# Own places for modulation rows in an FFN output, a new product order, and gate sums in place, in a two-layer diffusion step

## The chip, the cores and the metric

The kernel runs on one core of one Trainium2 chip. The metric is the device time of one execution in microseconds (us), as a median over several runs. The kernel before took 1518.62 us (three runs, 1517.99 to 1518.99).

A core has five engines with queues of their own, each worked off in order. TensorE multiplies matrices (PE in the profile; PEld is its weight load, which overlaps). VectorE (DVE) does element-wise work with two operands, ScalarE (ACT) copies and activation functions, GpSimd (POOL) side work, and SyncE (SP) issues transfers. POOL issues transfers too, on a queue of its own. Engines wait for each other through semaphores. SBUF is the on-chip memory from which the engines work, PSUM the eight banks into which TensorE accumulates.

## The reference

Two layers run over 512 latent tokens and 128 prompt tokens (640 together, T), with a model width of 1024 (D). Layer 0 mixes with MLA heads and neighbourhood attention, layer 1 with grouped-query attention (GQA, 8 heads). After each mixer comes a SwiGLU FFN with a hidden width of 2816. A condition vector scales, shifts and gates every sub-layer; there are two conditions, one for the latent and one for the prompt tokens:

```python
m = silu(cond) @ w_mod[l] + b_mod[l]          # 6 x 1024: sh1 sc1 g1 sh2 sc2 g2
h  = rms_norm(x, norm_mix[l]) * (1 + sc1) + sh1
x  = x + g1 * mixer(h)
h  = rms_norm(x, norm_ffn[l]) * (1 + sc2) + sh2
gate, up = split(h @ w_ffn_in[l], 2)
x  = x + g2 * ((silu(gate) * up) @ w_ffn_out[l])
```

The output is the final RMS norm of x for both groups, and the context tensors of each layer.

## The kernel before

**Precision and layout.** Activations lie transposed: features on the 128 partitions, the 640 tokens along the free dimension, in two halves of 320 (HT). Weights and activations are split into a high and a low part (ScalarE copies the high part, VectorE subtracts it for the low part), and a product is three matmuls: high x high, high x low, low x high (`mm3`). So every weight tile costs a load, a ScalarE pass and a VectorE pass before TensorE can finish with it.

**FFN input** (`ffn`, from L1238, the loop from L1497). The hidden width has 22 blocks (fb) of 128. After the first two blocks, each block is one step of a seven-product scheme for two-by-two block matrices (halves of the features, halves of the tokens), with sums of weights (X, Y, Z, W, built from the gate weights g and the up weights u by the class `Weights`) and sums of activations (D, N, C, E, built by `ModS`). TensorE's order in a block is X x first half, D, E of the block before, N, X x second half, Z, C; VectorE follows with `up`, `g` (a PSUM sum that must be read before E adds to that bank), the weight sums s, the low parts and the gating. In layer 0, from block 5 on (QUICK), the transfer itself adds the two halves of the gate weights; for blocks 2 to 4 VectorE adds them. Gate weights of blocks 2 to 4 are loaded into `rawp`, later ones into tiles with the tag "wr" (two buffers, 1536 columns in layer 0), which before that hold normalised activations of `ModS`.

**FFN output.** Part one (from L1608) handles the first ten hidden blocks for the eight output blocks n of 128 features; the three hidden blocks that never left SBUF run ahead for n = 0 to 3. Each n then has two jobs (`jobs`, L1645), and `prepare` loads, splits and queues the weights of the next job (`wout`, L1608). The raw weights go in turn into `rawp` (three buffers) and into one buffer in the pool fo. Part two (from L1677) handles the other twelve hidden blocks in six pairs, again with seven products for each pair p of output blocks: S2, A11, S3, A12 and A22 for the left (first) half of the tokens and S1 and S4 for the right. The weight sums S1 and S2 lie in tiles of fo with the tags "S1" and "S2" (768 columns). PLAN is TensorE's order, MAKE that in which weights are made, three products ahead. The activations of the hidden pairs (kinds T1 to T4, B11, B21, B22) were spilled to DRAM; `later` are those fetched during part one, the rest follows into `spots` as the buffers of part one come free.

**Modulation rows.** Most of the modulation is not done by TensorE. `left` lists 56 rows of 128 output features; for each, 512 KB of weights are fetched and VectorE multiplies them with the two conditions (two instructions "junk", L1841, of 1024 columns, with a running sum). `mod_side` spreads these rows over the kernel as side work: its plan gives the number of rows for each stage, "o" in the mixer's output projection (after each output block), "fb" in the FFN input (after each block) and "n" in the FFN output part one. `fetch` takes the next rows and issues their loads (SP's queue in the FFN input and in the heads, POOL's queue elsewhere); the next `step` queues their products on VectorE behind the instruction it is given, then fetches the rows for the next step. Without a place of its own, a row's raw weights take one of the three buffers of `rawp`, which the weights use too. In the GQA heads, `gside.ask(1)` (L2120) brings one row to a head.

**Order of the work.** The kernel is written for a scheduler that fixes each engine's instruction order when it is built; the program's order and `after`/`issue_after` constrain it. On the chip an engine runs its queue in that order, and an instruction that waits holds up all behind it. A buffer's next user waits for its last reader.

Of the kernel before, what the change touches and what calls it, by code (L numbers as in the profile page):

```python
# [11 lines left out]
F32 = mybir.dt.float32  # L12
# [6 lines left out]
P = 128  # L19
# [31 lines left out]
def body(ctx, tc, xT, vecs, wm0, wm0g, wm1, wA, wNV, wNA, wMK, wMV, wOA, wGQ, wGK, wGV, wOC,  # L51
# [1186 lines left out]
    def ffn(l, x, pend, hm, nxt, side, opened):  # L1238
# [98 lines left out]
        def fetch_g(fb):  # L1337
            if fb >= FB:
                return
            g = wFI[l, fb, 0]  # L1340
            if fb == FEW or l == 0 and fb < QUICK:
                raws[fb, 0] = load(g, 1024, f"wg{l}_{fb}r")
                return
            t = raws[fb, 0] = fp.tile([P, WR[l]], F32, tag="wr", bufs=2, name=f"wg{l}_{fb}r")
            if l == 1:
                nc.sync.dma_start(t, g)
                return
            y = t[:, :1024].rearrange("p (a b) -> p a b", a=2)

            def from_(at, step):  # L1350
                return bass.AP(tensor=g.tensor, offset=g.offset + at, ap=[list(g.ap)[0], [step, 2], [1, 512]])
            nc.sync.dma_start(y, from_(0, 0))
            nc.gpsimd.dma_start(y, from_(512, P * 1024 - 512), accum_op=ALU.add)
            nc.sync.dma_start(t[:, 1024:], g[:, 512:])

        class Weights:

            def __init__(self, fb):
                self.fb = fb
                self.u, g = raws[fb, 1], raws[fb, 0]  # L1360
                self.g0, self.g, self.s13 = g[:, :512], g[:, 512:1024], None
                if l == 0 and fb >= QUICK:
                    self.g, self.s13 = g[:, 1024:], g[:, :1024]
                self.X = wX[fb - FEW] if fb < FEW + AHEAD else None

            def sums(self):
                ru, s13 = self.u, self.s13
                if s13 is None:
                    tag, n, bufs = ("ws", 1024, 2) if l else ("w4", 1024, 2) if self.fb == FEW else ("wr", WR[0], 2)
                    s13 = fp.tile([P, n], F32, tag=tag, bufs=bufs, name=f"s13{l}_{self.fb}")[:, :1024]  # L1370
                    dve(V.tensor_tensor, s13[:, :512], self.g0, self.g, ALU.add)
                    dve(V.tensor_tensor, s13[:, 512:], ru[:, :512], self.g0, ALU.add)
                s24 = fp.tile([P, 1024], F32, tag="ws", bufs=1 + l, name=f"s24{l}_{self.fb}")
                dve(V.tensor_tensor, s24[:, :512], s13[:, 512:], self.g, ALU.add)
                dve(V.tensor_tensor, s24[:, 512:], s24[:, :512], ru[:, 512:], ALU.add)
                self.s = {"X": ru, "Y": s13, "Z": s24}
                self.t = {c: wtile(f"w{c}{l}_{self.fb}") for c in "XYZ" if c != "X" or self.X is None}
# [218 lines left out]
        later = [(c, i) for c in ("T2", "B11", "T1", "B22") for i in range(len(PAIRS))]  # L1596
# [7 lines left out]
        def some(n):  # L1604
            for _ in range(min(n, len(later))):
                fetch_kind(*later.pop(0), fo, "hd")

        def wout(j0, n, tiles, name):  # L1608
# [12 lines left out]
            V.tensor_tensor(t[:, 1, :m], raw[:, :m], f(t[:, 0, :m]), ALU.subtract)  # L1621
# [30 lines left out]

        prepare(0)
        step("n", -1)
# [17 lines left out]
        def evac(n, c, ps):  # L1672
# [7 lines left out]
        PLAN = [(p, c) for p in (0, 1) for c in ("S2", "A11", "S1", "S3", "S4", "A12", "A22")] + \  # L1680
            [(p, c) for p in (2, 3) for c in LEFT] + [(p, c) for p in (2, 3) for c in RIGHT]
        MAKE = [(p, c) for p in (0, 1) for c in ("S2", "A11", "S1", "S3", "A22", "S4", "A12")] + \
            [(p, c) for p in (2, 3) for c in ("S2", "A11", "S3", "A22", "A12")] + [(p, c) for p in (2, 3) for c in RIGHT]
# [9 lines left out]
        def source(p, c):  # L1693
            n = 2 * p
            r = raw.setdefault(p, {})
            if c == "S2":
                for w, m, j, pool in (("A21", n + 1, 0, rawp), ("A22", n + 1, 1, fo), ("A11", n, 0, rawp), ("A12", n, 1, rawp)):
                    r[w] = get(w, m, (len(FIRST) + j * len(PAIRS)) * P, pool)
                if p == 3:
                    wide = fk.tile([P, 2 * D], F32, tag="cb", bufs=1, name=f"wide{l}")  # L1700
                    r["S1"], r["S2"] = wide[:, :M], wide[:, M:2 * M]
                else:
                    for w in ("S1", "S2"):
                        r[w] = fo.tile([P, M], F32, tag=w, bufs=1, name=f"wo{l}_1_{n}{w}")
# [42 lines left out]
        for c in ("T3", "B21", "T4"):  # L1747
            for i in range(len(PAIRS)):
                tag, pool = spots.pop(0)
                fetch_kind(c, i, pool, tag)  # L1750
        order = iter(range(KT))
        ended = prev = None
        for j, (p, c) in enumerate(PLAN):
# [19 lines left out]
            elif c == "S3":  # L1773
                V.tensor_tensor(t["u3"], ps, t["p1"], ALU.add)
                if not late:
                    V.tensor_tensor(t["u3"], b[p]["c"][:, :HT], t["u3"], ALU.add)
                    evac(n + 1, 1, t["u3"])
                elif l == 1 and p == 3:
# [11 lines left out]
            elif c == "S1":  # L1790
# [3 lines left out]
                if late:  # L1794
                    V.tensor_tensor(t["u3"], ps, t["u3"], ALU.add)
                    ended = evac(n + 1, 1, t["u3"])
# [18 lines left out]
    def mod_side(plan):  # L1815


        def start(pool, place=None):
# [4 lines left out]
            def fetch(n, queue=nc.sync):  # L1823
# [28 lines left out]
            def step(kind, at, behind=None):  # L1852
# [9 lines left out]
                if kind != "fb":  # L1862
                    fetch(plan(kind, at + 1), nc.gpsimd)
# [4 lines left out]
            step.ask = ask  # L1868
# [8 lines left out]
    def x_again(n):  # L1877
# [8 lines left out]
                        mod_side(lambda kind, i: (1, 1, 1, 1, 0)[i])(op[1], wide(op, 0)))  # L1886
    box2, nxt = next_mod("h10", gs[1][0], mods[1], SH1, even=((0, 1, 2, 4, 5, 7), (0, 2, 5)))
    side = mod_side(lambda kind, i: (i > 3) + 2 * (i == FB - 1) if kind == "fb" else 2 * (i < 7))
# [231 lines left out]
    for h in range(8):  # L2120
        if h in (2, 3, 4, 5, 6):
# [202 lines left out]
```

## Time and profile before

| | us |
|---|---|
| median of 3 runs | 1518.62 (1517.99 to 1518.99) |
| the profiled execution, device time | 1516.8 |
| its span in the profile | 1515.0 |
| TensorE busy | 1444.8 |
| VectorE busy | 1231.5 |
| ScalarE busy | 788.7 |
| GpSimd busy | 216.2 |

The profile is of one execution. A line of the view by group or in time names engine, source line, operation and tiles (`out<-in`); in the view of waits, "A <- B: total, times, longest" is the time that engine A stood still until B released it. In the view by stretches each row is a stretch of time, its length, the busy time and instruction count of each engine, the granted TensorE clock (1.00 is full), the share of time that the transfer engines were busy and what they moved. The chain of work lists start, length and what was done on the path that ended last. In an issue line, the last number is the median time from issue to landing.

Layer 0's mixer output runs at about 320 to 372 us, its FFN input to 657, its FFN output to 838; GQA's heads follow to about 1020, and layer 1's FFN takes 1075 to 1505.

### The profile page before, as it was taken

How to read it: one execution, taken by the hardware profiler on the slowest of the kernel's cores; microseconds unless marked ns; L12 is line 12 of the kernel's file. 1: busy time of each engine (PE TensorE's matmuls, PEld its weight loads, DVE VectorE, ACT ScalarE, POOL GpSimd, SP SyncE). 2: the span in 40 equal slices, each digit the busy share in tenths (PEclk: the TensorE clock that was granted, in tenths of full speed). 3: DMA queues.
4: the chain of work that ended last, by engine and by line, in shares of the span. 5: the costliest groups of instructions: out<-in, count | busy, mean ns of one | idle time of the engine just before them, and what ended most of it. 6: DMA issues, size and time to landing. Idle time of an engine off the chain costs nothing.

```text
span 1515.0 us, 25965 instructions
## 1 busy us (share of the span) xinstructions
PE 1444.8 (95%) x9715; PEld 1389.9 (92%) x9715; DVE 1231.5 (81%) x2324; ACT 788.7 (52%) x1571; POOL 216.2 (14%) x328
## 2 busy tenths in 40 slices
PE   5999999999999999987999999999999999999997
PEld 4989878889999999986889998989999999999997
DVE  5686788878989999957678888886889999963486
ACT  5455678853755555521134666673655555542254
POOL 0335625411000000000000322220000000000000
PEclk9999999999999999998999999999999999999999
DMA  9544420044189999888562220224245555569531
GB/s 370 209 148 164 148 84 15 29 175 140 57 271 268 268 285 271 265 295 286 163 215 90 104 74 31 71 81 161 74 162 182 187 190 203 187 210 317 180 126 70
DMA packets 96383, 258.53 MB, mean 171 GB/s; under 512 B 10400, under 2 KB 16512, under 8 KB 95488
## 3 DMA queue, kind: packets, MB, share of 16 engines
q1 hardware_dynamic: 85392, 228.51, 44.1%
q0 software_dynamic: 9664, 26.31, 6.9%
q10 hardware_dynamic: 1200, 2.05, 0.4%
q8 instruction: 76, 1.25, 0.3%
q14 instruction: 51, 0.42, 0.1%
HBM read 215.71 MB, written 41.12 MB: 170 GB/s over the span
## 4 chain that ended last, share of the span: by engine, by line
PE 73%; DVE 14%; ACT 5%; DMA 4%; issue 3%; SPq 0%; DVEq 0%; POOL 0%; ACTq 0%; POOLq 0%
PE fg L63 18%; PE fd L63 9%; PE fu L63 4%; PE fo L63 3%; PE gq L63 2%; PE nk L63 2%; PE nq L63 2%; DVE junk L1841 2%; PE fo_0b L63 1%; PE gs L63 1%; PE fo_2b L63 1%; PE go L63 1%; PE fo_0a L63 1%; PE fo_1b L63 1%; PE fo_2a L63 1%
## 5 line engine op out<-in xcount | busy, mean ns | idle before, releaser
L1841 DVE SCALAR_TENSOR_TENSOR junk<-wm,cb 128x1024 bf16<-128x1024 f32 x112 | 137.4, 1227 | 1.4
L1261 ACT ACTIVATE sg<-g 128x320 f32<-128x320 f32 x28 | 13.2, 472 | 103.4 <-DVE g L1261 103.4
L63 PE MATMUL gq<-h10h,wgq 128*128 128x320 f32 x256 | 66.9, 318 | 0.1
L1261 DVE TENSOR_TENSOR wZ<-s,wZ 128x1024 fp32r<-128x1024 f32 x40 | 48.8, 1219 | 0.0
L63 PEld LDWEIGHTS gq<-h10h,wgq 128*128 128x128 f32 x256 | 45.0, 188 | 1.0 <-PE gtp L67 0.3
L63 PE MATMUL fg<-h01E,wW 128*128 128x320 f32 x240 | 40.2, 318 | 5.4 <-DVE g L1261 5.4
L1261 ACT ACTIVATE wZ<-s 128x1024 fp32r<-128x1024 f32 x40 | 42.2, 1055 | 1.6 <-DVE s L1261 1.5
L63 PEld LDWEIGHTS fg<-h01E,wW 128*128 128x128 f32 x240 | 37.3, 195 | 6.0 <-DVE g L1261 5.9
L63 PE MATMUL gq<-h10l,wgq 128*128 128x320 f32 x128 | 39.5, 308 | 0.0
L63 PE MATMUL fg<-h01C,wY 128*128 128x320 f32 x240 | 38.6, 309 | 0.9 <-ACT u L1261 0.9
L63 PE MATMUL fg<-h01q,wX 128*128 128x320 f32 x240 | 39.3, 309 | 0.0
L63 PE MATMUL fd<-h01q,wZ 128*128 128x320 f32 x240 | 38.7, 309 | 0.5 <-ACT p L1261 0.5
L63 PE MATMUL fu<-h01q,wX 128*128 128x320 f32 x240 | 39.2, 309 | 0.0
L2035 ACT ACTIVATE gp<-gs,gb,rq 128x640 f32<-128x640 f32 (+1 forms) x40 | 31.9, 797 | 13.9 <-DVE gb L2034 13.8
L63 PE MATMUL fd<-h11q,wZ 128*128 128x320 f32 x240 | 38.6, 309 | 0.4 <-ACT p L1261 0.4
L63 PE MATMUL fg<-h01N,wZ 128*128 128x320 f32 x240 | 38.9, 310 | 0.0
L63 PE MATMUL fd<-h01D,wY 128*128 128x320 f32 x240 | 38.6, 309 | 0.2 <-DVE wY L1261 0.2
L63 PE MATMUL fg<-h11E,wW 128*128 128x320 f32 x240 | 38.7, 310 | 0.0
L63 PE MATMUL fg<-h11q,wX 128*128 128x320 f32 x240 | 38.6, 309 | 0.0
L63 PE MATMUL fg<-h11N,wZ 128*128 128x320 f32 x240 | 38.6, 309 | 0.0
L63 PE MATMUL fu<-h11q,wX 128*128 128x320 f32 x240 | 38.6, 309 | 0.0
L63 PE MATMUL fg<-h11C,wY 128*128 128x320 f32 x240 | 38.5, 309 | 0.0
(2821 smaller groups left out, 5129.9 us busy)
## 6 DMA issues: line engine op xcount, KB each, us to landing
hr_T<-sp_T SPq DMA_DIRECT2D x48, 320.0 KB, 6.5
wm<-in_wm SPq DMA_DIRECT2D x29, 512.0 KB, 4.7
hr_B<-sp_B SPq DMA_DIRECT2D x36, 320.0 KB, 6.1
wm<-in_wm POOLq DMA_DIRECT2D x19, 512.0 KB, 4.4
mraw<-in_wm SPq DMA_DIRECT2D x8, 1024.0 KB, 15.5
mraw<-in_wm SPq DMA_DIRECT2D x16, 512.0 KB, 4.0
cb<-crs SPq DMA_DIRECT2D x6, 1024.0 KB, 6.3
mrow<-in_wm0g POOLq DMA_DIRECT2D x8, 512.0 KB, 6.3
```

Of the source, the lines that this page charges most:

```text
L63: cls.last = nc.tensor.matmul(*a, **k)
L1261: self.last = after(self.last, lambda: op(*a, **k))
L1841: last = V.scalar_tensor_tensor(junk, raw, 1.0, cb[:, c, :], ALU.mult, ALU.mult, accum_out=mods[l][:, j0 + i, c:c + 1])
L2035: weighed.append((S.activation(dst, src, AF.Exp, bias=nb, scale=rq[:, j:j + 1], accum_out=ll[:, j:j + 1]), v))
```

## The change

Four edits go together.

1. Modulation rows that are fetched in the first FFN output (part one) no longer use `rawp`; each takes the tile tagged S1 or S2 of the pool fo in turn, which is enlarged to 1024 columns for that. Two rows are fetched before the first job's weights, and their products stand behind those weights' low part, so that part one now handles 16 rows rather than 14. The plans move rows: in layer 0's mixer output none for the first step and two for the last (four as before); in the FFN input the last block's three become one, and blocks 5 and 6 get two each; GQA's heads 2 and 6 lose theirs.
2. In part two the left products of a pair come first for all pairs, not only for the last two: PLAN, MAKE, the order in which spilled kinds are fetched, and the place where the right half's sum u3 is finished.
3. The gate weights of blocks 3 and 4 in layer 0 are loaded into the last 1024 columns of a wr tile, and VectorE writes their sums into its first 1024 columns, in place of a second tile. They leave `rawp`.
4. GQA's heads that carry a row are 3, 4 and 5.

```diff
-            if fb == FEW or l == 0 and fb < QUICK:
+            if fb == FEW:
                 raws[fb, 0] = load(g, 1024, f"wg{l}_{fb}r")
                 return
             t = raws[fb, 0] = fp.tile([P, WR[l]], F32, tag="wr", bufs=2, name=f"wg{l}_{fb}r")
-            if l == 1:
-                nc.sync.dma_start(t, g)
+            if l == 1 or fb < QUICK:
+                nc.sync.dma_start(t[:, -1024:], g)
                 return
...
-                if l == 0 and fb >= QUICK:
-                    self.g, self.s13 = g[:, 1024:], g[:, :1024]
+                if l == 0 and fb > FEW:
+                    self.g0, self.g, self.s13 = g[:, 512:1024], g[:, 1024:], g[:, :1024]
...
                 if s13 is None:
-                    tag, n, bufs = ("ws", 1024, 2) if l else ("w4", 1024, 2) if self.fb == FEW else ("wr", WR[0], 2)
-                    s13 = fp.tile([P, n], F32, tag=tag, bufs=bufs, name=f"s13{l}_{self.fb}")[:, :1024]
+                    s13 = fp.tile([P, 1024], F32, tag="ws" if l else "w4", bufs=2, name=f"s13{l}_{self.fb}")
+                if l == 1 or self.fb < QUICK:
                     dve(V.tensor_tensor, s13[:, :512], self.g0, self.g, ALU.add)
                     dve(V.tensor_tensor, s13[:, 512:], ru[:, :512], self.g0, ALU.add)
...
-        later = [(c, i) for c in ("T2", "B11", "T1", "B22") for i in range(len(PAIRS))]
+        later = [(c, i) for c in ("T2", "B11", "T3", "B21") for i in range(len(PAIRS))]
...
-            V.tensor_tensor(t[:, 1, :m], raw[:, :m], f(t[:, 0, :m]), ALU.subtract)
+            low[0] = V.tensor_tensor(t[:, 1, :m], raw[:, :m], f(t[:, 0, :m]), ALU.subtract)
...
+        step.place = lambda name: fo.tile([P, D], F32, tag=f"S{1 + len(left) % 2}", bufs=1, name=name)
+        step("n", -2)
         prepare(0)
-        step("n", -1)
+        step("n", -1, low[0])
...
-        PLAN = [(p, c) for p in (0, 1) for c in ("S2", "A11", "S1", "S3", "S4", "A12", "A22")] + \
+        PLAN = [(p, c) for p in (0, 1) for c in LEFT + RIGHT] + \
             [(p, c) for p in (2, 3) for c in LEFT] + [(p, c) for p in (2, 3) for c in RIGHT]
-        MAKE = [(p, c) for p in (0, 1) for c in ("S2", "A11", "S1", "S3", "A22", "S4", "A12")] + \
-            [(p, c) for p in (2, 3) for c in ("S2", "A11", "S3", "A22", "A12")] + [(p, c) for p in (2, 3) for c in RIGHT]
+        MADE = "S2", "A11", "S3", "A22", "A12"
+        MAKE = [(p, c) for p in (0, 1) for c in MADE + RIGHT] + [(p, c) for p in (2, 3) for c in MADE] + \
+            [(p, c) for p in (2, 3) for c in RIGHT]
...
-                        r[w] = fo.tile([P, M], F32, tag=w, bufs=1, name=f"wo{l}_1_{n}{w}")
+                        r[w] = fo.tile([P, D], F32, tag=w, bufs=1, name=f"wo{l}_1_{n}{w}")[:, :M]
...
-        for c in ("T3", "B21", "T4"):
+        for c in ("T4", "T1", "B22"):
...
                 V.tensor_tensor(t["u3"], ps, t["p1"], ALU.add)
-                if not late:
-                    V.tensor_tensor(t["u3"], b[p]["c"][:, :HT], t["u3"], ALU.add)
-                    evac(n + 1, 1, t["u3"])
-                elif l == 1 and p == 3:
+                if l == 1 and p == 3:
...
-                if late:
-                    V.tensor_tensor(t["u3"], ps, t["u3"], ALU.add)
-                    ended = evac(n + 1, 1, t["u3"])
+                V.tensor_tensor(t["u3"], ps, t["u3"], ALU.add)
+                ended = evac(n + 1, 1, t["u3"])
...
-            def fetch(n, queue=nc.sync):
+            def fetch(n, queue=nc.sync, place=place):
...
-                    fetch(plan(kind, at + 1), nc.gpsimd)
+                    fetch(plan(kind, at + 1), nc.gpsimd, step.place)
...
-                        mod_side(lambda kind, i: (1, 1, 1, 1, 0)[i])(op[1], wide(op, 0)))
+                        mod_side(lambda kind, i: (0, 1, 1, 2, 0)[i])(op[1], wide(op, 0)))
...
-    side = mod_side(lambda kind, i: (i > 3) + 2 * (i == FB - 1) if kind == "fb" else 2 * (i < 7))
+    side = mod_side(lambda kind, i: (i > 3) + (i in (5, 6)) if kind == "fb" else 2 * (i < 7))
...
-        if h in (2, 3, 4, 5, 6):
+        if h in (3, 4, 5):
             extra = named("m", gside.ask(1))
```

More of the change, by code (lines that the diff above doesn't have):

```diff
@@ L1606, in some @@
                 fetch_kind(*later.pop(0), fo, "hd")
+        low = [None]
         def wout(j0, n, tiles, name):
@@ L1867, in ask @@
                 return list(ops())
-            step.ask = ask
+            step.ask, step.place = ask, place
             if place is not None:
```

## The prediction

> **What bounds the kernel now.** I read the page first, then TensorE's waits, then the busy time by stage. The page:
>
> ```profile
> span 1515.0 us, 25965 instructions
> PE 1444.8 (95%) x9715; PEld 1389.9 (92%) x9715; DVE 1231.5 (81%) x2324; ACT 788.7 (52%) x1571; POOL 216.2 (14%) x328
> ```
>
> TensorE (PE) is busy for 95%, and the change removes none of its matmuls. What can be won is its waiting, and the time in which its clock is not fully granted. Its waits, from the view of waits:
>
> ```profile
> PE fo_2a L63 <- ACT wo L1620: 6.2, 1, 6.2
> PE fg L63 <- DVE g L1261: 5.4, 1, 5.4
> ...
> PE fo_4a L63 <- ACT wo L1620: 4.6, 1, 4.6
> ...
> PE fo_1b L63 <- ACT wo_1S L1726: 2.6, 2, 2.4
> PE oa3a L63 <- DVE oaw L185: 1.9, 1, 1.9
> PE fo L63 <- ACT wo L1620: 1.6, 2, 1.4
> PE fo_6a L63 <- ACT wo L1620: 1.6, 1, 1.6
> ...
> PE gkp L63 <- DVE gr_4r L385: 1.4, 1, 1.4
> PE fo_1b L63 <- DVE wo_1S L1727: 1.4, 2, 0.7
> ```
>
> Nearly all stand in the FFN output of layer 0. Layer 1 runs the same code there without modulation rows, so it is a control. The next two lines reach from the last FFN-input product (E) to the first product of output part two (S2), in layer 0 and layer 1 (columns: length, then busy time and count of PE, PEld, DVE, ACT, POOL; granted clock, DMA share, GB/s):
>
> ```profile
> 662.20:758.00 95.80, 80.83 (x494) 78.28 (x494) 59.55 (x105) 17.97 (x26) 7.53 (x14) 0.90 0.71 243
> 1356.90:1428.40 71.50, 71.50 (x489) 71.50 (x489) 28.78 (x47) 15.99 (x23) 0.00 (x0) 1.00 0.69 240
> ```
>
> The same matmuls take 24.3 us longer with rows: about 15 us of waits and, at a clock of 0.90, about 9.5 us of slow matmuls. One matmul at full clock is 71.5/489 = 0.146 us. How it happens, from VectorE (DVE) in time and the chain of work:
>
> ```profile
> 653.73 1.22 DVE L1841 SCALAR_TENSOR_TENSOR junk<-wm,cb 128x1024 bf16<-128x1024 f32 x1
> ...
> 660.06 1.23 DVE L1841 SCALAR_TENSOR_TENSOR junk<-wm,cb 128x1024 bf16<-128x1024 f32 x1
> ...
> 661.70 0.48 DVE L1261 TENSOR_TENSOR g<-fg,p 128x320 f32<-128x320 f32 x1
> ...
> 690.09 0.08 DVE L1841 DVE_READ_ACCUMULATOR junk<-wm,cb 128x1 f32 x1
> ```
>
> ```profile
> 690.20 5.27 DMA wo_23r<-in_wFO
> ```
>
> Six row products (three rows, two conditions each) stand ahead of g in the last input block: 653.73 to 661.2. Later the weight load wo_23 is issued at 690.20, right when a row product ends: the row held one of rawp's three buffers. It lands 5.27 us later, and fo_2a has waited 6.2 us.
>
> **Last input block of layer 0.** One row is left there in place of three. Two products end near 656.3, up follows, and g is done at about 657.2; the product before E ended at 656.8 (662.2 less the 5.4 us wait). About 0.4 us of the wait stays: gain 5.0. At worst none (the output's first weights come late instead), at best 5.4.
>
> **Output part one of layer 0.** Rows get two places in the pool fo, so rawp serves weights alone, as in layer 1. Rows rise from 14 to 16: 32 products.
>
> ```profile
> L1841 DVE SCALAR_TENSOR_TENSOR junk<-wm,cb 128x1024 bf16<-128x1024 f32 x112 | 137.4, 1227 | 1.4
> ```
>
> ```profile
> wm<-in_wm POOLq DMA_DIRECT2D x14, 512.0 KB, 5.1
> ```
>
> ```profile
> 730.32 0.53 POOL L1830 DMA_DIRECT2D wm<-in_wm  x1 [4.42 <-DVE junk L1841]
> ```
>
> ```profile
> 1374.83 0.68 DVE L331 SCALAR_TENSOR_TENSOR lead<-fo_0b,mods,lead 128x192 f32<-128x192 f32 x2 [1.20 <-PE fo_0b L63]
> ...
> 1416.82 0.96 DVE L1706 TENSOR_TENSOR wo_0S<-wo_0S,wo_0A11r 128x768 f32<-128x768 f32 x1
> ```
>
> VectorE's own work in layer 1's stage is 28.8 us; 32 x 1.23 = 39.4 us more make 68 of 71.5. It fits, but barely. A place turns over in 2.5 us (two products) + 0.5 (issue on POOL's queue) + 5.1 (landing) = 8.1 us, two rows a turn. TensorE's output blocks n take 42 x 0.146 = 6.1 us up to n = 3 (three of ten hidden blocks ran ahead; six matmuls for each), then 60 x 0.146 = 8.8. The first block's residual ends 18.6 us into the stage (1375.5 less 1356.9). Six turns and the last four products give 18.6 + 48.6 + 5.0 = 72.2. The places are the tiles of the sums S1 and S2 that part two begins with: sum, high part and low part, 3 x 0.96 = 2.9 us by the row of the sum, follow. S2's product starts at 75.1, a new wait of 3.6 us; were the blocks the limit (row products from 63.3), it would be none. Low parts of other weights queue on VectorE behind row products that wait for a landing; I leave two waits as the present fo and fo_6a, 3.2 us (bounds 0 and 17, rivals below). Stage: 71.5 + 3.6 + 3.2 = 78.3, a gain of 17.5 (8 to 24).
>
> **Part two.** In layer 0 the second pair's weights stand late:
>
> ```profile
> 775.38 0.96 DVE L1705 TENSOR_TENSOR wo_2S<-wo_3A21r,wo_3A22r 128x768 f32<-128x768 f32 x1 [0.95 <-DMA wo_3A22r<-in_wFO]
> ```
>
> ```profile
> 780.13 3.98 PE fo_1b L63 x16
> ```
>
> The fo_1b waits are 4.0 us over both layers, 2.4 + 0.7 = 3.1 of them here; the 16 matmuls behind them take 3.98 in place of 2.34 (clock), 1.6 more. With part one's loads as early as in layer 1, its 0.9 us remains: gain 3.8 (0 to 4.7). Left products first hand back the raw buffers of A21, A22 and A12 one to three weights sooner, for both layers; in layer 1 that touches 0.9 us, of which I take 0.4. T4, T1 and B22 are now the tiles fetched last, needed as fifth to seventh product; T3, B21 and T4 were fourth, sixth and seventh, so that edit alone costs nothing unless the loads start later than now.
>
> **Mixer output of layer 0.** No row is due after the first two blocks.
>
> ```profile
> 339.83 1.22 DVE L1841 SCALAR_TENSOR_TENSOR junk<-wm,cb 128x1024 bf16<-128x1024 f32 x1
> ...
> 341.44 1.22 DVE L185 TENSOR_TENSOR oaw<-oaw3r,oaw 128x1024 fp32r<-128x1024 f32 x1
> ```
>
> ```profile
> 342.70 5.02 PE oa3a L63 x22
> ```
>
> ```profile
> 345.00:350.00 5.00, 5.00 (x28) 5.00 (x28) 3.56 (x7) 0.47 (x1) 0.53 (x1) 0.75 0.53 186
> ```
>
> Two products, 2.4 us, leave the queue ahead of oaw3's low part, and its wait of 1.9 us goes. The 22 matmuls of oa3a behind it took 5.02 where 3.2 is full speed: 1.8 more. Two rows fall together after block 4, ahead of oaw7's low part; I charge 0.5. Gain 3.2 (0.5 to 3.7). The Trainium skill ("TensorE: Matmul & The Clock Gate", part 1) says that the clock halves only after an idle window of about 3.4 us; by it the wait of 1.9 us costs no clock, and the sum would be 1.8 us smaller. The granted clock of 0.75 right behind that wait speaks against it.
>
> **Input of layer 0, against the gain.** Blocks 5 and 6 take two rows each, 2.5 us more apiece ahead of g, and E must follow g.
>
> ```profile
> 460.90 0.48 DVE L1261 TENSOR_TENSOR g<-fg,p 128x320 f32<-128x320 f32 x1
> ...
> 472.01 0.48 DVE L1261 TENSOR_TENSOR g<-fg,p 128x320 f32<-128x320 f32 x1
> ```
>
> ```profile
> 462.72 3.52 PE fg L63 x24
> ...
> 475.04 3.52 PE fg L63 x24
> ```
>
> Slack is 1.3 us in block 5 and 2.5 in block 6; 5.0 us of products leave a loss of 2.5 (0 to 5: rows also hold rawp buffers, and on SP's queue the next gate weights stand behind them).
>
> The early gate sums: wg_3 and wg_4 leave rawp for the two wr tiles, which hold normalised activations until their last use.
>
> ```profile
> 414.66 0.48 DVE L325 TENSOR_TENSOR h01E<-h0132d,h01E 128x320 fp32r<-128x320 f32 x1
> ...
> 419.86 0.69 DVE L1261 TENSOR_TENSOR s<-wg_3r 128x512 f32<-128x512 f32 x1
> ...
> 427.85 0.69 DVE L1261 TENSOR_TENSOR s<-wg_4r 128x512 f32<-128x512 f32 x1 [0.88 <-DMA wg_4r<-in_wFI]
> ```
>
> ```profile
> 423.24 4.58 DMA wg_4r<-in_wFI
> ```
>
> Freed at 415.1, wg_3 lands 4.58 us later, at 419.7, just before its sum; wg_4's 0.88 us of waiting goes. Gain 0.7 (-1.5 to 1.5).
>
> **Heads.** Two rows fewer: of gkp's wait of 1.4 us, behind a row product of head 2, I take 1.0 (0 to 2.5).
>
> **Sum:** 5.0 + 17.5 + 3.8 + 0.4 + 3.2 - 2.5 + 0.7 + 1.0 = 29.1 us. The profiled execution took 1516.8 (1.8 us around its span), so 1487.7. The runs' median, 1518.6, stands 1.8 above it: 1489.5.
>
> **Rivals.** *The transfers set the stage.* For: with rows, TensorE stood still while the engines moved all they could, and the stretch 648 to 760 moved 28 MB:
>
> ```profile
> 690.00:695.00 5.00, 0.00 (x0) 0.00 (x0) 3.74 (x9) 0.63 (x1) 0.53 (x1) 0.72 1.00 370
> ```
>
> ```profile
> DMA packets 11466, 28.13 MB, mean 251 GB/s; under 512 B 1248, under 2 KB 2272, under 8 KB 11460
> ```
>
> About 27 MB must move between 648 and S2. At 370 GB/s that is 73 us, S2 at 721, no limit; at 270 it is 100 us, S2 at 748, 12.5 us behind my 735.5 (657.2 + 78.3): 1502. The Trainium skill ("DMA: Bandwidth & Descriptors", Queues, rings and completion order) says that the engines alternate between queues packet by packet, so POOL's rows would take half whenever one is in flight: 18.7 MB on SP's queue at 185 GB/s, 101 us, S2 at 749. No run here shows such a split. Chance 0.12.
>
> *Row products ahead of each block's second low part.* VectorE works in order: residual 0.7, four products 5.0 and a low part 0.7 are 6.4 us, where the block's first job covers 18 x 0.146 = 2.6 (then 4.4). Three times 3.8 and three times 2.0 are 17, in place of my 3.2, and 4 for the clock: 1507. Against: now, too, there are four a block. Chance 0.08.
>
> *Full cover.* Handover, part one and blocks 5 and 6 cost nothing: 1489.5 - 3.6 - 3.2 - 2.5 = 1480. Chance 0.11.
>
> *Slower: the two places throttle VectorE.* If a row takes over 11.0 us to land, a turn exceeds 14.0 and the stage 18.6 + 6 x 14.0 + 5.0 + 2.9 = 110.5; against 95.8 that eats the other 11.6 us of gain and 3 more. At 13 us: 122.5, total 1534. A row takes 5.1 now, with the engines full. Chance 0.06.
>
> *It does not do what it says:* the new places come free only with the last input tiles, the first rows land late in front of the hidden block's split, and handover and clock take the rest: no change, 1516 to 1521. Chance 0.05.
>
> **The numbers.** My forecast, 1484 to 1498, has 0.58. 0.2% is 3 us, about what can be told apart. Faster: 0.58 + 0.12 + 0.08 + 0.11 = 0.89; same 0.05; slower 0.06. The range from full cover to the rival of the low parts, 1479 to 1508, leaves out about two in ten with the tails.
>
> **What the changed profile would show.** Right: fo_2a, fo_4a and fg gone from the waits; layer 0's stage near 78 us at a clock near 1.0; row products without SP's weight loads behind them; a new wait of about 4 us before S2; small waits of fg on g in blocks 5 and 6. Wrong: VectorE waiting long for wm, weight loads landing in over 8 us, or a stage over 90 us.

## The result, and the profile after

| | before | after |
|---|---|---|
| median, us | 1518.30 (4 runs, 1516.10 to 1518.99) | 1498.72 (4 runs, 1495.80 to 1502.75) |
| the profiled execution, us | 1516.8 | 1497.84 |
| its span, us | 1515.0 | 1496.1 |

The change makes the kernel faster: the ratio is 0.9875, with a 95% interval of 0.9849 to 0.9901, a gain of 19.6 us by the medians and 18.9 us by the spans. The forecast was a gain of 29.1 us, to 1489.5 us: the direction holds, and the gain is two thirds of what was forecast. The median lies 0.7 us outside the forecast's own range (1484 to 1498) and inside the wide one (1479 to 1508).

The page of the changed kernel:

```profile
span 1496.1 us, 25964 instructions
...
PE 1439.0 (96%) x9715; PEld 1384.7 (93%) x9715; DVE 1229.1 (82%) x2324; ACT 787.9 (53%) x1571; POOL 215.1 (14%) x330
```

TensorE's waits:

```profile
PE fo_0b L63 <- ACT wo_0S L1731: 11.7, 1, 11.7
...
PE fo L63 <- DVE wo L1623: 2.1, 1, 2.1
PE fo_6a L63 <- DVE wo L1623: 1.6, 1, 1.6
...
PE fo_0b L63 <- DVE wo_0S L1732: 1.4, 1, 1.4
```

fo_2a (6.2), fo_4a (4.6) and fg on g (5.4) are gone. In their place stands one wait of 11.7 + 1.4 = 13.1 us, of fo_0b: S2's product, the first of output part two. The stage from the last FFN-input product (E) to S2, which took 95.8 us before:

```profile
655.65:746.53 90.88, 74.04 (x488) 72.84 (x486) 63.89 (x116) 16.26 (x24) 7.97 (x15) 0.92 0.91 324
```

The forecast for it was 78.3. Nine matmuls of the output (1.3 us), which stood behind E before, now run ahead of it, so the like-for-like length is about 92.2. The chain of work shows what the stage consists of (pieces under 2.8 us left out):

```profile
654.37 8.17 DMA wm<-in_wm
...
662.58 2.84 issue
665.43 5.00 DMA wm<-in_wm
...
670.47 10.74 issue
681.22 7.22 DMA wm<-in_wm
...
688.51 3.30 issue
691.82 7.91 DMA wm<-in_wm
...
703.23 6.25 DMA wm<-in_wm
...
709.52 3.52 issue
713.06 4.16 DMA wm<-in_wm
...
720.72 4.09 DMA wm<-in_wm
...
724.85 3.45 issue
728.32 6.68 DMA wm<-in_wm
...
746.53 4.63 PE fo_0b L63 x16
```

Loads of rows (wm) alternate with the time until the next issue on POOL ("issue", or the pieces left out), in which VectorE makes the two products of the row that landed: the turn of the two places is itself the path that ends last. The rows' landing and the first sum of part two:

```profile
DMA to landing us min/median/max: 3.7/6.7/8.3
```

```profile
741.00 0.95 DVE L1710 TENSOR_TENSOR wo_0S<-wo_1A21r,wo_1A22r 128x768 f32<-128x768 f32 x1
```

TensorE has finished its blocks at 732.5; the last row products end at 740.9, and only then can VectorE make S1 and S2, in the very tiles that the rows held. The 16 matmuls behind the wait took 4.63 us, where they took 2.63 before.

**Where the 18.9 us come from.** Both kernels run 9715 matmuls. The table gives TensorE's lead at the same matmul of its sequence: the start of matmul number N in the trace of before, less its start in the other trace. A lead that rises between two marks is time won there. The last column is the step's forecast.

| up to matmul (its start before, us) | lead of after | won in the step | forecast |
|---|---|---|---|
| 2100 (333.8), ahead of every edit | 0.5 | 0.5 | 0 |
| 2300 (366.8), mixer output of layer 0 | 3.9 | 3.4 | 3.2 |
| 2900 (458.3), early gate sums | 4.7 | 0.7 | 0.7 |
| 4240 (655.3), input blocks 5, 6 and on | 2.3 | -2.4 | -2.5 |
| 4249 (662.2), last input block, to E | 7.9 | 5.6 | 5.0 |
| 4730 (755.3), output part one | 24.6 | 16.7 | 21.1 |
| 4760 (760.6), handover to S2 | 9.4 | -15.2 | -3.6 |
| 4960 (795.1), part two of layer 0 | 14.0 | 4.6 | 3.8 |
| 6500 (1029.2), GQA heads | 17.4 | 3.4 | 1.0 |
| 9714 (1506.1), layer 1 | 18.0 | 0.6 | 0.4 |

The span differs by 1.0 more, behind the last mark. At 4249 the changed kernel has the nine matmuls of the output ahead of E: 1.3 of the 5.6 us there belong to part one. Up to the end of part one the steps come near their forecast, part one itself 4.4 us below it (the forecast of 17.5 for the stage is 21.1 less the handover's 3.6); the handover takes 15.2 us back.

### The profile page after: what moved, and what is told of

The parts are those of the page before. It is cut to its first block, busy times and chain, and to the rows that moved or that the text cites. A ratio compares the mean times of both kernels' runs of the same rounds, so it can differ in the third digit from the quotient of the medians.

```text
span 1496.1 us, 25964 instructions
## 1 busy us (share of the span) xinstructions
PE 1439.0 (96%) x9715; PEld 1384.7 (93%) x9715; DVE 1229.1 (82%) x2324; ACT 787.9 (53%) x1571; POOL 215.1 (14%) x330
## 4 chain that ended last, share of the span: by engine, by line
PE 59%; DVE 20%; ACT 8%; issue 7%; DMA 6%; DVEq 0%; SPq 0%; POOL 0%; ACTq 0%; POOLq 0%
PE fg L63 10%; PE fd L63 5%; DMA wm<-in_wm 3%; PE gq L63 3%; PE fo L63 2%; PE fu L63 2%; DVE junk L1842 2%; PE nk L63 2%; PE nq L63 2%; PE gs L63 2%; PE fo_0b L63 1%; PE fo_2b L63 1%; DVE wY L1261 1%; PE go L63 1%; PE mod L63 1%
## 5 line engine op out<-in xcount | busy, mean ns | idle before, releaser
L1842 DVE SCALAR_TENSOR_TENSOR junk<-wm,cb 128x1024 bf16<-128x1024 f32 x112 | 137.4, 1227 | 18.0 <-DMA wm<-in_wm 16.8
L63 PE MATMUL fg<-h01q,wX 128*128 128x320 f32 x240 | 42.5, 309 | 0.0
L2036 ACT ACTIVATE gp<-gs,gb,rq 128x640 f32<-128x640 f32 (+1 forms) x40 | 31.9, 797 | 17.4 <-DVE gb L2035 17.2
L63 PE MATMUL fd<-h11D,wY 128*128 128x320 f32 x240 | 38.4, 308 | 0.0
```

The costliest lines, as they stand in the source:

```text
L63: cls.last = nc.tensor.matmul(*a, **k)
L1842: last = V.scalar_tensor_tensor(junk, raw, 1.0, cb[:, c, :], ALU.mult, ALU.mult, accum_out=mods[l][:, j0 + i, c:c + 1])
L2036: weighed.append((S.activation(dst, src, AF.Exp, bias=nb, scale=rq[:, j:j + 1], accum_out=ll[:, j:j + 1]), v))
```

## The experiments

**Theory.** The turn of the two places paces the rows: two products, POOL's issue, and a landing that other transfers stretch. The last rows end behind TensorE's blocks, and S1 and S2 wait for them. **Rivals:** the transfers of the stage as a sum; VectorE's work as a sum; the product order as the source of the gain. The experiments change the changed kernel, unless said otherwise. Leads compared between runs are rises over one step, since the lead ahead of every edit already differs by -3.2 to 0.5 us from run to run.

### One turn fewer: e1_heads_five

```diff
-    side = mod_side(lambda kind, i: (i > 3) + (i in (5, 6)) if kind == "fb" else 2 * (i < 7))
+    side = mod_side(lambda kind, i: (i > 3) + (i in (5, 6)) if kind == "fb" else 2 * (i < 6))
...
-        if h in (3, 4, 5):
+        if h in (2, 3, 4, 5, 6):
```

> The changed kernel with one plan taken back: part one of layer 0's FFN output carries 14 rows in place of 16, and GQA's heads 2 and 6 carry the other two again. Theory (the turn of the two places sets the end of part one, and S1 and S2 wait for the last products): the last turn, 7.6 us by its issues (720.72 to 728.32), is gone, S2's product starts about 7.6 us sooner, the waits of fo_0b fall from 13.1 to about 5.5 us; the heads lose the 3.8 us of TensorE's lead that they won. Net 3.8 faster than the changed kernel: 1495. Rival (the transfers set the stage): 1 MB less of some 29, about 2.6 us sooner at 390 GB/s, less 3.8 in the heads: 1500.

Measured: 1490.96 us (5 runs, 1488.21 to 1491.78), ratio to the kernel before 0.9818 [0.9795, 0.9841]: 7.8 us faster than the changed kernel. The wait of S2's product and the sum S1:

```profile
PE fo_0b L63 <- DVE wo_0S L1732: 0.9, 1, 0.9
```

```profile
730.15 0.96 DVE L1710 TENSOR_TENSOR wo_0S<-wo_1A21r,wo_1A22r 128x768 f32<-128x768 f32 x1
```

The handover costs 0.7 us of lead in place of 15.2. The sum starts 10.9 us sooner (741.00 to 730.15), more than the 7.6 of one turn by its issues: the last pair of rows is issued 8.5 us sooner (719.8 for 728.3) and its first row lands in 4.5 us in place of 6.7, ahead of the transfers of T4, T1 and B22. The slow clock behind the wait goes too. The heads win nothing and lose 1.9 us, where after wins 3.4: two rows there cost 5.3. Of this, 1.5 is slow clock behind a wait of 2.1 us (gs) that cost no clock in the kernel before. The theory holds, with its size too small; the transfers' rival (2.6 us) falls. This version beats both kernels.

### Two turns fewer, rows in the FFN input: e2_rows_twelve

```diff
-    side = mod_side(lambda kind, i: (i > 3) + (i in (5, 6)) if kind == "fb" else 2 * (i < 7))
+    side = mod_side(lambda kind, i: (i > 3) + (i in (5, 6, 7, 8, 9, 10)) if kind == "fb" else 2 * (i < 5))
```

> The changed kernel with 12 rows in part one of layer 0's FFN output in place of 16; the other four stand in blocks 7 to 10 of the FFN input, two rows each as in blocks 5 and 6. Theory (turn of the places): the last two turns go, 15.2 us by their issues; the row products end near 726, before TensorE has done its blocks at 732.5; the wait before S2 falls from 13.1 to 0 to 2 us; blocks 7 to 10 cost 0 to 1.2 us each, as 5 and 6 did (2.4 together), taken at 2.4 together. About 12 us faster than the changed kernel: 1487. Rival (transfers): 2 MB less, 5.2 us, less 2.4: 1496. Rival (VectorE's total work in the stage): four rows are 9.8 us of products, less 2.4: 1491.

Measured: 1502.25 us (6 runs, 1501.39 to 1503.79), ratio 0.9897 [0.9879, 0.9916]: a miss, 3.5 us slower than the changed kernel by the medians (the ranges overlap), where 12 us faster was expected.

```profile
PE fg L63 <- DVE g L1261: 8.0, 7, 3.3
PE fo_1b L63 <- ACT wo_1S L1731: 3.5, 1, 3.5
```

The handover is won as expected (a rise of 0.9 at S2 in place of -15.2). But from matmul 2900 to 4240 the lead falls by 12.6 us, where after loses 2.4: four rows cost 10.2, 2.5 each, the full time of their products on VectorE. Blocks 5 and 6 had slack; 7 to 10 have none. And the second pair now waits for its weights: from matmul 4760 to 4960 the lead falls by 5.1 where after wins 4.6, another 9.7 us. This part is not the rows' own work: in SP's queue two of that pair's weight loads now stand ahead of the 18 transfers of T4, T1 and B22, which are issued from 744.2 on (727.3 in after), and a third, wo_3A22, stands behind them at 759.1; VectorE waited 7.6 us for it.

### No landing, and short products: e3_no_loads, e4_short_products

```diff
+        same = {}
...
+            if k in same:
+                return same[k], True
...
-                    queue.dma_start(raw, src)
...
+                    if not there:
+                        queue.dma_start(raw, src)
```

> The changed kernel, with 14 of part one's 16 row loads left out: all 32 products run at full length on the two rows that were loaded first, so layer 1's modulation is computed from other weights. What goes is the landing in the turn and 7.3 MB of transfers; VectorE's work stays. Theory (turn): the waits of fo_0b (13.1 us) fall below 2, S2's product starts 12 to 15 us sooner; about 1485. Rival (transfers): the same. Rival (VectorE's work in its order is too much): the wait stays near 13 and VectorE is busy up to S2's sum; 1497.

```diff
-                            last = V.scalar_tensor_tensor(junk, raw, 1.0, cb[:, c, :], ALU.mult, ALU.mult,
+                            w = 64 if step.place is not place else D
+                            last = V.scalar_tensor_tensor(junk[:, :w], raw[:, :w], 1.0, cb[:, c, :w], ALU.mult, ALU.mult,
```

> The changed kernel, with part one's 32 row products cut from 1024 to 64 columns (the rest of each sum is left out, so the modulation is not the whole one); all loads, places and waits stay. Theory (turn): a turn falls by the 2.5 us of products to issue and landing, about 7.2, so seven turns end some 15 us sooner; the wait before S2 goes, and with it the low parts' small waits; about 1483. Rival (VectorE's work): the same. Rival (transfers set the stage): nothing is moved less, S2's product starts within 3 us of where it did; 1496 to 1499.

Measured: e3 1482.57 us (2 runs, 1482.31 to 1482.84), ratio 0.9765 [0.9733, 0.9798]; e4 1480.47 us (2 runs, 1477.66 to 1483.28), ratio 0.9752 [0.9716, 0.9787]. TensorE's waits in e3:

```profile
PE fo_0b L63 <- ACT wo_0S L1739: 1.7, 1, 1.7
PE fo_0b L63 <- DVE wo_0S L1740: 1.0, 1, 1.0
```

With all of VectorE's work but no landing (e3), the wait falls from 13.1 to 2.7 (below 2 was expected); with all transfers but short products (e4) it is gone. So neither VectorE's sum of work nor the transfers' sum sets the stage; each is harmless without the other. What is left is the turn in which they follow one another.

### Places alone, on the kernel before: e5_places_alone

```diff
+        step.place = lambda name: fo.tile([P, D], F32, tag=f"S{1 + len(left) % 2}", bufs=1, name=name)
         step("n", -1)
...
-                        r[w] = fo.tile([P, M], F32, tag=w, bufs=1, name=f"wo{l}_1_{n}{w}")
+                        r[w] = fo.tile([P, D], F32, tag=w, bufs=1, name=f"wo{l}_1_{n}{w}")[:, :M]
...
-                    fetch(plan(kind, at + 1), nc.gpsimd)
+                    fetch(plan(kind, at + 1), nc.gpsimd, step.place)
```

> The kernel before with one part of the change: rows of part one take the tiles S1 and S2 (enlarged to 1024 columns) in place of rawp; plans (14 rows, three in the last input block, five heads) and product order stay. Theory (what matters is when the last rows are done, against the end of TensorE's blocks): its first rows are fetched one step later than in the first experiment, so the last two stand behind the seventh block as in the changed kernel; the waits of fo_2a and fo_4a go (about 14 us of lead in part one, as measured for the change), and a wait before S2 of 10 to 13 us, with slow clock behind it, takes 12 to 15 of it back; with some 4 us in the second pair: 1512 to 1517. Rival (the number of rows matters, 14 against 16): no wait before S2, 13 us in the stage and 4 in the second pair: 1501.

Measured: 1509.05 us (4 runs, 1505.37 to 1510.71), ratio 0.9946 [0.9926, 0.9966].

```profile
PE fo_0b L63 <- ACT wo_0S L1727: 12.0, 1, 12.0
```

Fourteen rows, and the wait is there all the same, since the last two are fetched one step later than in e1: their place in time decides, not their number. The lead rises by 20.0 us in part one (expected 14) and falls by 14.6 at the handover, so the time is 3 us better than the range that was expected. The mixer output, whose edit is not in this kernel, wins nothing here (-0.1).

### The order: e6_order_undone

```diff
-        PLAN = [(p, c) for p in (0, 1) for c in LEFT + RIGHT] + \
+        PLAN = [(p, c) for p in (0, 1) for c in ("S2", "A11", "S1", "S3", "S4", "A12", "A22")] + \
...
-        later = [(c, i) for c in ("T2", "B11", "T3", "B21") for i in range(len(PAIRS))]
+        later = [(c, i) for c in ("T2", "B11", "T1", "B22") for i in range(len(PAIRS))]
```

> The changed kernel with the order of part two taken back (PLAN, MAKE, the kinds that are fetched late, the place of u3), all else as changed. Theory: the 4.5 us that TensorE gains between S2 and the end of the second pair come from part one's loads being out of the way, not from the order; the time stays within 1.5 us: 1497 to 1500. Rival (left products first hand the raw buffers back sooner, and that gives the gain): the second pair waits for its weights as in the kernel before; 4 to 5 us slower: 1503.

Measured: 1497.13 us (4 runs, 1495.92 to 1499.37), ratio 0.9872 [0.9854, 0.9890]. The lead rises by 4.8 us from matmul 4760 to 4960, with the changed order by 4.6. The order is worth nothing that can be measured; that rival falls.

### What stretches the landing: e7_kinds_held, e9_all_kinds_held

```diff
+            if held:
+                V.tensor_copy(t[:, 0:1], raw[0]["S1"][:, 0:1])
...
-                fetch_kind(c, i, pool, tag)
+                fetch_kind(c, i, pool, tag, l == 0 and (c, i) == ("T4", 0))
```

In e9 the other 17 transfers are put behind the first as well:

```diff
-                fetch_kind(c, i, pool, tag)
+                first = after(first, lambda: fetch_kind(c, i, pool, tag, l == 0 and (c, i) == ("T4", 0))) if first is None else (
+                    after(first, lambda: fetch_kind(c, i, pool, tag)) and first)
```

> The changed kernel, with the 18 transfers of T4, T1 and B22 (5.9 MB) held on SP's queue until VectorE has made the sum S1 of the first pair; one cast of one column is added for that. In the changed kernel they are issued from 727.3 on, beside the last two rows (issued 728.3 and 730.9, landed some 7 us later). Theory (the turn of the last rows is stretched by those transfers): the last rows land in 4 to 5 us, S2's product starts 3 to 5 us sooner; T4 is needed some 20 us behind S2 and just in time: 1494 to 1497. Rival (the last turn costs the same without them): S2 starts where it did, T4 lands later: 1499 to 1503.

Measured: 1497.03 us (4 runs, 1496.07 to 1498.75), ratio 0.9871 [0.9854, 0.9888]. It decides nothing: only the first tile was held, the scheduler put seven others ahead of it in SP's queue, and the last rows still landed in 7.3 us.

> The changed kernel with all 18 transfers of T4, T1 and B22 behind the first pair's sum S1, now in their order as well (in e7_kinds_held seven of them were issued ahead of the one that was held, and the engines still moved 400 GB/s while the last rows landed in 7.2 us). Theory (SP's traffic stretches the last rows' landing): the last two rows land in 4 to 5 us, the products end 2 to 4 us sooner, the wait of fo_0b falls from 13.1 to 9 to 11 us; if T4, issued some 3 us ahead of S2's product and needed 21 us behind it, comes in time, 1494 to 1497. Rival (the landing of two rows on POOL's queue is long by itself): the wait stays at 12 to 14 us; 1498 to 1502.

Measured: 1502.44 us (4 runs, 1499.44 to 1503.27), ratio 0.9904 [0.9885, 0.9922]. The rows issued between 728 and 745 in e9:

```profile
DMA packets 561, 1.82 MB, mean 107 GB/s; under 512 B 64, under 2 KB 64, under 8 KB 561
...
wm<-in_wm POOLq DMA_DIRECT2D x2, 512.0 KB, 3.9
```

The same stretch of after:

```profile
DMA packets 2584, 6.35 MB, mean 373 GB/s; under 512 B 282, under 2 KB 282, under 8 KB 2584
...
wm<-in_wm POOLq DMA_DIRECT2D x2, 512.0 KB, 7.0
```

The same two rows land in 3.9 us when little else moves, in 7.0 when SP's transfers run beside them. (The 107 GB/s are a mean over 17 us, and the rows were in flight for the first 8 of them.) S2's wait falls to 8.6 us:

```profile
PE fo_0b L63 <- ACT wo_0S L1734: 8.0, 1, 8.0
PE fo_1b L63 <- ACT wo_1S L1734: 4.1, 1, 4.1
...
PE fo_0b L63 <- DVE wo_0S L1735: 0.6, 1, 0.6
```

The theory holds for the landing and misses the time, which is 3.7 us above the changed kernel's by the medians: three of the second pair's four weights stand in SP's queue behind the held transfers (issued at 757 to 759; in after at 746 to 749), and fo_1b waits for them.

### Late prefetch: e10_late_prefetch, e11_fourteen_late, e12_prefetch_held

e10, and e11 on the kernel of e1:

```diff
-                if n > 1:
-                    some(4)
+                if n > 4:
+                    some(8)
```

e12:

```diff
-            nc.sync.dma_start(f(t), solo[c, i])
+            if l == 0 and (c, i) == ("T2", 0):
+                V.tensor_copy(t[:, 0:1], x[3][:, 0:1])
+            d = after(first[0], lambda: nc.sync.dma_start(f(t), solo[c, i]))
...
-                if n > 1:
-                    some(4)
+                if n > (2 if l == 0 else 1):
+                    some(5 if l == 0 else 4)
```

> The changed kernel with the 24 transfers of T2, B11, T3 and B21 (7.9 MB), four after each of the blocks 2 to 7, moved to eight after each of the blocks 5 to 7. Theory (SP's traffic sets the landing, and the landing the turn): the turns that took 10.6, 11.4 and 9.8 us between 681 and 713, with the engines full, fall to 7.5 to 8.5, as the last two were; the rows end 4 to 8 us sooner unless the moved transfers stretch the last turns by as much: 1492 to 1498, landing of the middle rows 4 to 5 us. Rival (the transfers' sum sets the stage): the same bytes in less time, T2 or B11 late at S2; 1502 to 1508. Rival (the landing is POOL's own): no change, 1498.

> The first experiment's kernel (14 rows in part one, five heads with a row) with the late prefetch of e10_late_prefetch. S2 has no wait for the rows there, so only the waits of fo and fo_6a for low parts (4.2 us with their clock behind them) can shrink. Theory: the rows end sooner and the low parts with them: 1488 to 1491. Rival (the transfers' sum): T2, B11 and the weights of the second pair come late: 1494 to 1500.

Measured: e10 1498.05 us (4 runs, 1495.38 to 1501.09), ratio 0.9885 [0.9863, 0.9907]; e11 1491.81 us (4 runs, 1487.12 to 1493.04), ratio 0.9832 [0.9810, 0.9854]. Neither tests its theory: in e10's trace these transfers are issued from 659.5 to 696.5, as they are from 659.8 to 698.2 in after, and in e11's from 662.8 to 701.3. The lines moved in the program, the loads did not move in SP's queue.

> The changed kernel with the 24 transfers of T2, B11, T3 and B21 truly held: the first waits for a cast of one column behind the fourth block's residual (some 703 us), the others follow it in SP's queue. In e10_late_prefetch the edit moved nothing: the scheduler issued them at 659 to 697 as before. Theory (SP's traffic sets the landing, the landing the turn): the rows between 669 and 700 land in 4 to 5 us in place of 6.5 to 8, the turns of 10.6 and 11.4 us fall to 8 to 9; the later ones, with 7.9 MB more beside them, rise from 7.7 to 9 or 10; the time within 4 us of the changed kernel, 1495 to 1503. Rival (a row's landing is POOL's own, whatever SP moves): the landing stays at 6 to 8 us between 669 and 700.

Measured: 1495.85 us (4 runs, 1493.54 to 1499.01), ratio 0.9854 [0.9828, 0.9880]. Transfers of 660 to 700 in e12, and in after:

```profile
DMA packets 3791, 9.90 MB, mean 248 GB/s; under 512 B 427, under 2 KB 788, under 8 KB 3787
...
wm<-in_wm POOLq DMA_DIRECT2D x8, 512.0 KB, 4.1
```

```profile
DMA packets 5730, 13.85 MB, mean 346 GB/s; under 512 B 640, under 2 KB 921, under 8 KB 5728
...
wm<-in_wm POOLq DMA_DIRECT2D x6, 512.0 KB, 7.2
```

At 248 GB/s a row lands in 4.1 us, at 346 in 7.2. The turns in e12, by POOL's issues 679.50, 686.62, 694.37 and 702.71, are 7.1, 7.8 and 8.3 us; from there, with 386 to 405 GB/s moving in all up to 720, 10.5 (713.17) and 9.7 (722.84). The theory holds, and the rival that a landing is POOL's own falls. The time cannot be told from the changed kernel's, since most of the wait moves from S2 to fo_6a:

```profile
PE fo_6a L63 <- DVE wo L1628: 7.0, 1, 7.0
PE fo_6a L63 <- ACT wo L1627: 2.8, 1, 2.8
PE fo_0b L63 <- ACT wo_0S L1736: 2.6, 1, 2.6
```

### Rows in the mixer output: e8_rows_in_mixer

```diff
-                        mod_side(lambda kind, i: (0, 1, 1, 2, 0)[i])(op[1], wide(op, 0)))
+                        mod_side(lambda kind, i: (0, 2, 2, 2, 0)[i])(op[1], wide(op, 0)))
...
-    side = mod_side(lambda kind, i: (i > 3) + (i in (5, 6)) if kind == "fb" else 2 * (i < 7))
+    side = mod_side(lambda kind, i: (i > 3) + (i in (5, 6)) if kind == "fb" else 2 * (i < 6))
```

> The changed kernel with 14 rows in part one of layer 0's FFN output in place of 16; GQA's heads keep three rows as changed, and the two others stand in layer 0's mixer output, whose plan becomes 0, 2, 2, 2, 0. Theory: part one as in the first experiment (no wait before S2, some 12.5 us against the changed kernel), heads as in the changed kernel (3.8 us of lead); two more rows in the mixer output cost 0 to 2.5 us each, as the two rows after block 4 did little there (3.4 of 3.7 us of gain were left). 1486 to 1491, taken 1488. Rival (a row costs VectorE's 2.5 us wherever it stands on a full engine): 5 us lost in the mixer, 1491 as in the first experiment.

Measured: 1492.64 us (5 runs, 1491.17 to 1496.13), ratio 0.9843 [0.9824, 0.9863].

```profile
PE fd L63 <- DVE wY L1261: 2.7, 1, 2.7
...
PE oa6a L63 <- DVE oaw L185: 2.4, 1, 2.4
```

From matmul 2100 to 2900 it loses 3.9 us where after wins 4.2: two rows cost 8.1 here, more than in the heads and more than the rival's 5. Only 2.5 of it falls up to matmul 2300, in the mixer output; the other 5.6 falls in the first input blocks behind it, where fd waits for wY. Among the kernels that compute everything e1 has the lowest median; e8 and e11 lie within 2 us of it.

## Why the prediction was right in direction and short in size

**The step that failed** is "Six turns and the last four products give 18.6 + 48.6 + 5.0 = 72.2", with S2's product (75.1) and its new wait of 3.6 us worked out from it. Counted from E (655.65), the last product ended at 740.9, that is 85.3, 13.1 us later, and S2's product started at 90.9, 15.8 later. Four parts make it up.

*The first turn (4.5 us).* The first issue behind a row of block 0 came at 681.22, 25.6 into the stage, where 18.6 + 2.5 = 21.1 was taken. VectorE works in order and stood on another weight's low part in between; that weight's load, issued at 672.50, took 5.8 us to land:

```profile
679.09 0.69 DVE L1623 TENSOR_TENSOR wo<-wo_26r,wo 128x512 fp32r<-128x512 f32 x1 [3.97 <-ACT wo L1622]
```

*The next five turns (6.6).* From 681.22 to 728.32 they took 10.6, 11.4, 9.8, 7.7 and 7.6, that is 47.1 in place of 5 x 8.1 = 40.5. The landings on this path (7.2, 7.9, 6.3, 4.2, 4.1) make 29.6 in place of 5 x 5.1 = 25.5. The other 17.5, in place of 5 x 3.0 = 15.0, lie between a landing and the next issue: in each of these turns a low part stands between the row's two products, which the turn of 8.1 had at nothing:

```profile
699.82 1.23 DVE L1842 SCALAR_TENSOR_TENSOR junk<-wm,cb 128x1024 bf16<-128x1024 f32 x1 [4.23 <-DMA wm<-in_wm]
...
700.97 0.82 DVE L1623 TENSOR_TENSOR wo<-wo_50r,wo 128x640 fp32r<-128x640 f32 x1
701.71 1.22 DVE L1842 SCALAR_TENSOR_TENSOR junk<-wm,cb 128x1024 bf16<-128x1024 f32 x1
```

*The last turn (2.0).* From the last pair's first issue to the end it took 12.6 in place of 0.5 + 5.1 + 5.0 = 10.6; its landing took 6.7.

*The sums (2.7).* From the last product to S2's product 5.6 us passed in place of 2.9: residuals, another sum and another weight's low part stand on VectorE between S1 and the low part of S2.

So the row's landing, taken as 5.1 us, is the largest single term that was mis-sized: about 5.7 of the 15.8 (4.1 and 1.6). Between 655 and 742 VectorE stood 16.8 us waiting for rows:

```profile
DVE junk L1842 <- DMA wm<-in_wm: 16.8, 8, 4.2
```

The 5.1 was the median of before, and it mixed two cases. In that trace the rows issued at 687.6 and 694.1, with 367 to 384 GB/s moving, landed in 7.3 and 7.0 us; those at 725.4 and 730.3, with 111 to 215, in 3.7 and 3.8. "A row takes 5.1 now, with the engines full" was therefore a wrong reading. In after the engines moved 351 GB/s up to 700 and 298 from there to S2, where the kernel before moved 318 and 178 in the two parts of its stage, and a row lands in 6.7 (e9 and e12: 3.9 and 4.1 with SP's transfers held, 7.0 and 7.2 otherwise). That SP runs ahead because rows no longer hold rawp's buffers is argued; no run tests it alone.

One more slip hid a part of the miss. The forecast adds 3.2 us of waits for low parts to the stage. By its own sum the rows set S2's start at 75.1, and TensorE's blocks with 3.2 us more would end at 74.7: these waits would have shortened the wait ahead of S2, not lengthened the stage, and the forecast would have been 3.2 us lower.

**The rivals.** "The transfers set the stage" gave S2 at 748 and 1502 us; measured 746.5 and 1498.7, near in number. That is luck: as a mechanism it falls, since e4 moves as many bytes and has no wait. The transfers act through the landing of the rows. The Trainium skill ("DMA: Bandwidth & Descriptors", Queues, rings and completion order) has the engines alternate between queues packet by packet; that a row slows down beside SP's traffic agrees with it (3.9 to 7.0 us). "The two places throttle VectorE" had the right mechanism, but 11.0 us of landing as the point from which it loses; the longest was 8.3. "Row products ahead of each block's second low part" is the small part: fo and fo_6a waited 2.1 + 1.6 = 3.7 us, forecast 3.2. Behind the first, 20 matmuls took 4.56 us in place of 20 x 0.146 = 2.9 (last section), 1.6 more. With the 0.5 and the 1.3 us of the nine matmuls that is 3.4 of the 4.4 us that part one lacks of its 21.1; the rest was not traced. "Full cover" in the output is what e4 shows, with most of each product left out.

**The terms that held.** Mixer output 3.4 (3.2), blocks 5 and 6 -2.4 (-2.5), and part two 4.6 (3.8), which e6 shows not to come from the order. The mixer's 3.4 stand against the rule that the prediction weighed there: by the Trainium skill ("TensorE: Matmul & The Clock Gate", part 1) the wait costs no clock, and the step would have given 1.4.

**Near in number only.** The last input block gave 5.6 (5.0), but not as forecast: E itself starts 4.3 us sooner, and g is done 1.1 us after the product before E. TensorE did not wait, because nine matmuls of the output now stand ahead of E, an order that the edits did not ask for. Layer 1 gave 0.6 (0.4), which the prediction put down to the order; e5 and e6, with the old order, win 0.6 and 0.4 there too, and the other runs lie between -0.5 and 1.1. The gate sums gave 0.7 (0.7); in the other runs with this edit up to matmul 2900 (e8 left aside) it was -0.1 to 0.7, so what it is worth is not settled.

**The heads** gave 3.4 where 1.0 was taken. The waits of before in 895 to 1035, and of after:

```profile
PE gs L63 <- ACT gp L2035: 2.7, 2, 2.1
PE gkp L63 <- DVE gr_4r L385: 1.4, 1, 1.4
```

```profile
PE gkp L63 <- ACT gtp1h L392: 0.2, 1, 0.2
```

The prediction saw only gkp; the 2.7 us of gs behind another head's row were overlooked. Both return in e1, with five rows.

## What to carry to other kernels

A landing is not a constant: take it from the part of the old trace that carries the traffic the changed kernel will have, not from a median over both kinds. When a side task paces itself by its own buffers, count everything that stands between its steps on the engine, not its own work alone. When those buffers belong to the next stage, work out when the last user leaves them, and let the last rows end before the main engine does: here one turn fewer was worth 7.8 us, though two rows had to go back to a dearer place. A load that should come later needs a wait of its own: moving its line in the program did not move it here, and a cast of one column did.

## What the runs showed of the hardware

Short waits did cost clock, but not every time, and their length alone does not decide it. In after, a wait of 2.1 us (up to 690.4) was followed by a granted clock of 0.66; in e10, one of 2.2 us (up to 716.3) by none:

```profile
685.00:690.00 5.00, 3.31 (x23) 3.04 (x21) 1.46 (x4) 0.71 (x2) 0.41 (x1) 1.00 1.00 379
690.00:695.00 5.00, 4.56 (x20) 4.57 (x21) 5.00 (x11) 1.37 (x2) 0.64 (x2) 0.66 0.87 248
```

```profile
715.00:720.00 5.00, 3.67 (x25) 3.67 (x26) 4.63 (x9) 0.00 (x0) 0.53 (x1) 1.00 0.73 208
720.00:725.00 5.00, 5.00 (x36) 5.00 (x35) 4.16 (x8) 1.47 (x2) 0.53 (x1) 1.00 0.48 183
```

The same wait of gs, 2.1 us long, left the clock at 1.00 in the kernel before (up to 1011.1) and took it to half in e1 (up to 984.2, slow from 985.6 to 989.0). A wait of 1.9 us cost clock ahead of oa3a in the kernel before (0.75) and none ahead of fo in e1 (up to 690.3). In after, before and e1 each of these slow stretches lasted 3.4 us. So a forecast that charges every short wait with 1.6 to 1.8 us of slow matmuls is right only some of the time. What decides is not settled here.
